# Small tiles padded to whole lines of 128 bytes, so that every tile in SBUF begins at a multiple of 128 bytes

## The chip, the core and the metric

The kernel runs on one core of one Trainium2 chip. The metric is the device time of one execution in microseconds (us); the median of three runs before the change is 1016.87 us. Engines carry the names of the profile: PE is TensorE's matmul stream, PEld its weight loads, DVE is VectorE, ACT is ScalarE, POOL is GpSimd, SP is the queue that issues the DMAs. For each matmul PE reads two operands from SBUF: the stationary one (128 columns, read by the weight load) and the moving one (256 or 512 columns, streamed through the array).

## What is computed

A transformer trunk of two layers on 256 rows of 1024 float32 channels. Each layer is a SwiGLU, a token mixer with 16 heads of three kinds, and a second SwiGLU, each with a norm before and after it:

```python
def swiglu(h, w_gate, w_up, w_down):
    return (jax.nn.silu(h @ w_gate) * (h @ w_up)) @ w_down

def reference(x, norm_gains, w_ffn_gate, w_ffn_up, w_ffn_down, w_in, w_out, diff_lambda, diff_subln_gain):
    for layer in range(DEPTH):
        g = norm_gains[layer]
        h = rmsnorm(x, g[0])
        x = x + 0.5 * rmsnorm(swiglu(h, w_ffn_gate[layer, 0], w_ffn_up[layer, 0], w_ffn_down[layer, 0]), g[1])
        h = rmsnorm(x, g[2])
        x = x + rmsnorm(token_mixer(h, w_in[layer], w_out[layer], diff_lambda[layer], diff_subln_gain[layer], layer), g[3])
        h = rmsnorm(x, g[4])
        x = x + 0.5 * rmsnorm(swiglu(h, w_ffn_gate[layer, 1], w_ffn_up[layer, 1], w_ffn_down[layer, 1]), g[5])
    return x
```

D_MODEL is 1024, D_FF is 2816. The four SwiGLUs hold 138 MB of the weights, the two mixers the rest of some 180 MB, all of it read from HBM once.

## The kernel before

**Weights.** `half` loads a piece of 128 x 1024 float32 into one of five buffers `raw`; ACT copies it into a float32r tile (`L271`, the high part) and DVE writes the difference into a second one (`L274`, the low part). The two tiles are one of ten `ring` buffers, here called ring0 to ring9; each takes its turn when it has been free for longest.

**Products.** A product of two float32 matrices is three matmuls (`mm3`): high by high, high by low, low by high, each with its own weight load. All matmuls come from one line of a helper, `mm`, `L356`, so the profile tells them apart by operands: `ps<-xt,ring` (rows `xt` moving, 256 columns, weights `ring` stationary: gate and up of a SwiGLU, queries and keys), `ps<-ring,xt` (weights moving, 256 columns, rows stationary: the first blocks of a SwiGLU, values), `ps<-ring,h` (weights moving, 512 columns, hidden values `h` stationary: down and the mixer's output). In a name of the profile the moving operand stands first.

**Order.** Each operation has a written-down duration; `Program.run` orders them for each engine by a list schedule before anything runs. The order is fixed in the program; only the semaphores' times differ from run to run.

**Where tiles lie.** Every tile is taken from one pool, `P1`, and gets an address at its first use, behind the tile before it. The program as built puts each at a multiple of 32 bytes and no more, so that a small tile such as `sm` (four float32 values, 16 bytes; 24 of them) shifts all the tiles behind it:

```python
    SM = Slots(P1, "sm", 24, [128, 4])
```

Addresses below are bytes from the start of a partition's row, as the program was built. A tile's row of 1024 float32 values is 4096 bytes, and all slices that PE reads begin at a multiple of 256 bytes from their tile's start, so the tile's start decides the slice's offset to a line.

Of the kernel before, what the change touches and what calls it, by code (L numbers as in the profile page):

```python
# [8 lines left out]
F32 = mybir.dt.float32  # L9
# [26 lines left out]
LAST_ORDER = ((9, 0), (6, 1), (10, 0), (7, 1), (8, 1), (9, 1), (10, 1))  # L36

C_IDENT, C_NEGU, C_NEG1, C_BLK, C_MASK = 0, 128, 256, 384, 512
C_BIAS = 768
# [29 lines left out]
class Slots:  # L69
    """Buffers of one kind (each one or more tiles); the one that has been free for longest goes first."""  # L70

# [12 lines left out]
class Buf:  # L84
    """A buffer from its first operation to its last one."""

# [12 lines left out]
class Program:  # L99
    """Operations with their dependencies, put in an order for each engine by a list schedule over  # L100
    estimated times (most urgent first), then traced in that order."""

# [119 lines left out]
def trunk(tc, x, norm_gains, w_gate, w_up, w_down, w_in, w_out, dlam, subln, consts, out):  # L222
# [16 lines left out]
    QS = Slots(P1, "q", N_QS, [128, 256])  # L239
    SM = Slots(P1, "sm", 24, [128, 4])  # L240
    GPO = Slots(P1, "gpo", 1, [128, D])
# [8 lines left out]

# [1 line left out]
    class Half:  # L252
# [4 lines left out]
    def half(pieces, cut=2):  # L257
        """Loads [128, 1024] and splits it exactly into two float32r parts."""
        h = Half()
        raw, h.ring = Buf(RAW), Buf(RNG, F32R)  # L260

        def load():
            for view, ap in pieces:
                nc.sync.dma_start(view(raw.t), ap)

        ld = op("DMA", 1.5, load, [prev[0]], [raw], lag=DMA_LAG)
        hi, lo = [], []
        w = 1024 // cut
        for s in (slice(w * c, w * (c + 1)) for c in range(cut)):
            def fhi(s=s):  # L270
                nc.scalar.activation(h.ring.t[0][:, s], raw.t[:, s], AF.Copy)  # L271

            def flo(s=s):
                nc.vector.tensor_tensor(h.ring.t[1][:, s], raw.t[:, s], h.ring.t[0][:, s].bitcast(F32), OP.subtract)  # L274

            hi.append(op("ACT", act_us(w, False), fhi, [ld] + hi[-1:] + last_hi, [raw, h.ring]))
            lo.append(op("DVE", dve_us(w), flo, [hi[-1]], [raw, h.ring]))
        last_hi[:] = hi[-1:]
        h.ready = lo
        prev[0] = ld  # L280
        return h
# [31 lines left out]

# [1 line left out]
    xs = P1.tile([128, 2, D], F32, name="xs")  # L315
    xr = x[0].rearrange("(t p) d -> p t d", p=128)
    cst = P1.tile([128, N_CONST], F32, name="cst")
    lamt = P1.tile([128, DEPTH, 4, 32], F32, name="lamt")
    gcol = P1.tile([128, DEPTH], F32, name="gcol")
    small = P1.tile([128, 2], F32, name="small")  # L320
    mhalf, epsc = small[:, 0:1], small[:, 1:2]
    nlam = P1.tile([128, DEPTH], F32, name="nlam")
    maskb = P1.tile([128, 256], BF16, name="maskb")
# [11 lines left out]
    def warm():  # L335
        """Work on zeros that brings the tensor engine to its full clock while the first loads run."""
        z, p = Buf(H2, BF16), Buf(PS)
        o = op("POOL", 0.2, lambda: nc.gpsimd.memset(z.t, 0.0), [], [z])

        def pe():  # L340
            for _ in range(N_WARM):
                mm(p.t, z.t[:, 0:128], z.t, True, True)

        op("PE", WARM_US, pe, [o], [z, p])
# [33 lines left out]

# [1 line left out]
    def sumsq(src, after, bufs, scale, psum):  # L380
        """Means of squares of the two halves of rows, in two columns."""
        v = Buf(SM)
        os = []
        for i in range(2):
            j = Buf(JK, BF16)

            def f(i=i, j=j):
                nc.scalar.activation(j.t, src(i), AF.Square, scale=scale, accum_out=v.t[:, i:i + 1])  # L388

            os.append(op("ACT", act_us(512, psum, 1), f, after[i], bufs[i] + [v, j]))  # L390
        return v, os
# [10 lines left out]
    def residual(T, accs, done, g, half_, final=False):  # L402
        """Norm of a sub-layer's output (token block T), added to the residual rows."""
        v, sq = sumsq(lambda i: accs[i].t, done, [[a] for a in accs], 1.0 / 16 if half_ else 1.0 / 32, True)
        r, orr = rstd(v, sq, 4 * EPS if half_ else EPS)
        res = []
        for i in range(2):
            y = Buf(ES)

            gb, gv, gl = g[i]  # L410

            def fy(i=i, y=y, gv=gv):
                nc.vector.tensor_tensor(y.t, accs[i].t, gv(), OP.mult)  # L413

            def fx(i=i, y=y):
                s = HALF[i]
                nc.vector.scalar_tensor_tensor(xs[:, T, s], y.t, r.t[:, 0:1], xs[:, T, s], OP.mult, OP.add)

            oy = op("DVE", dve_us(512), fy, done[i] + [gl], [accs[i], gb, y])
            ox = op("DVE", 0.66, fx, [oy, orr], [y, r])  # L420
            res.append(ox)
            if final:
                op("DMA", 0.8, lambda i=i: nc.sync.dma_start(out[0, TS(T), HALF[i]], xs[:, T, HALF[i]]), [ox])
        return res

    def normed(T, xo, g):
        """Normed rows of block T, in two halves."""
        v, sq = sumsq(lambda i: xs[:, T, HALF[i]], [[o] for o in xo], [[], []], 1.0 / 32, False)
# [12 lines left out]
    class XT:  # L441
        """Transposed normed rows in two float32r parts; done[T][b]: the ends for block T, chunk half b."""

# [31 lines left out]
    def wk(h, k):  # L475
        """Columns of contraction chunk k from two half tiles of 4 chunks each."""
        v = [t.rearrange("p (k c) -> p k c", k=4)[:, k % 4, :] for t in h[k // 4].ring.t]
        return v[0], v[1]
# [4 lines left out]
    def rows_op(p, c0, xt, T, hs, first):  # L483
        """p[:, c0:c0+256] = rows of block T times the 256 columns of tile hs; two steps."""
        o = None
# [7 lines left out]

# [1 line left out]
    def ffn(l, s, xt, na, turn1, g, final, nxt, pre):  # L495
        """turn1(): traces the second block's transposes; returns what follows the sub-layer."""
        wg, wu, wd = w_gate[l, s], w_up[l, s], w_down[l, s]
# [126 lines left out]

# [1 line left out]
    def mixer(l, xt, turn1, g, nxt, o_cst, o_misc):  # L626
# [22 lines left out]
        def qk(i):  # L649
            """Projects queries and keys of pair i, scaled, and splits both in two float32r parts.  # L650
            Differential pairs (4 maps of 32 channels): each map gets a tile with its two parts twice, in such
            an order that one pass over 128 partitions carries the four products. The others: the stationary
            side of head b has its high part on its own partitions and the low part on the other head's, the
            moving side its high part on both, so that two passes carry three products."""
            kind, n = PAIRS[i]
# [53 lines left out]
        def products(p, i, b, blocks, between=lambda: None):  # L709
            """Scores of head b of pair i; blocks: (output columns, stationary columns, moving columns)."""  # L710
            r = qk_[i]
            for n, (co, cs, cm) in enumerate(blocks):
                mm(p.t[:, co], r["s"][b].t[:, cs], r["m"][b].t[:, cm], n == 0)
            between()
            for co, cs, cm in blocks:
                mm(p.t[:, co], r["s"][b].t[HB[b], cs], r["l"].t[HB[b], cm], False, True)
# [4 lines left out]
        def scores(i, r0, n, h, den, d0):  # L721
            """exp(scores + bias - max) in rows, [block 1: keys 256 | block 0: keys 128], and the sums."""
            qk = qk_[i]
# [48 lines left out]
        def pair(i):  # L772
            """Generator: one stage at each next()."""
            kind, n = PAIRS[i]
# [18 lines left out]
            elif kind == "diff":  # L793
                es = []
                for b in range(2):
# [3 lines left out]
                    def comb(e1=e1, e2=e2, den=den, r=r):  # L799
                        nc.vector.reciprocal(r.t, den.t)  # L800
                        nc.vector.tensor_scalar(r.t[:, 2:4], r.t[:, 2:4], nlam[:, l:l + 1], None, OP.mult)
# [152 lines left out]

# [1 line left out]
    prev[0] = gp[0][2]  # L956
# [10 lines left out]
    def misc():  # L967
# [15 lines left out]
        pr = P1.tile([128, DEPTH, 2, 32], F32, name="pr")  # L983
        sm = P1.tile([128, DEPTH, 2], F32, name="sm")
        ex = P1.tile([128, DEPTH, 2], F32, name="ex")

# [4 lines left out]
        def f2():  # L991
            nc.vector.tensor_tensor(nlam, ex[:, :, 0], ex[:, :, 1], OP.subtract)
            for l in range(DEPTH):
# [63 lines left out]
```

## Time and profile before

| | |
|---|---|
| three runs | 1016.26, 1016.87, 1017.44 us |
| span of the profiled execution, first to last instruction | 1013.1 us |
| what lies around that span, by the median | 3.8 us |
| PE, PEld busy | 996.0, 923.9 us |
| DVE, ACT, POOL busy | 632.0, 581.9, 33.4 us |
| share of the chain that ended last: PE, ACT, DVE, DMA | 87%, 7%, 2%, 1% |
| DMA, mean | 181 GB/s, queue 59% busy |

Busy time of PE is the union of its matmuls' spans, from the start of one to its last result; neighbours overlap. How fast PE runs is seen in the distance from one matmul's start to the next, its pace, and that is read from rows of the timeline: the length of a row of n equal matmuls, less the duration of one, divided by n - 1. The core's mean granted TensorE clock was 0.998 of 2.4 GHz.

### The profile page before, as it was taken

The numbers are of one execution on the slowest core, as the hardware profiler recorded it, in microseconds if no ns is written. First come the engines' busy times: TensorE is split into PE (matmuls) and PEld (weight loads), VectorE is DVE, ScalarE is ACT, GpSimd is POOL, SyncE is SP. The second block draws the span as 40 slices with busy tenths as digits, with TensorE's granted clock in tenths as the row PEclk, the third lists the DMA queues.
The fourth block names the chain that finished last, engine by engine and source line by source line (L and its number), as shares of the span: only waits on it lengthen the run. The fifth ranks groups of instructions, "written<-read, shape, count | busy, mean of one in ns | idle before, by whom it ended". The sixth has DMA issues, their size and how long they took to land.

```text
span 1013.1 us, 18111 instructions
## 1 busy us (share of the span) xinstructions
PE 996.0 (98%) x7146; PEld 923.9 (91%) x7146; DVE 632.0 (62%) x1123; ACT 581.9 (57%) x1133; POOL 33.4 (3%) x58
## 2 busy tenths in 40 slices
PE   7999999999999999999999999999999999999997
PEld 6999999898888999999899999999998789999996
DVE  6755544778898745454685554448799776545433
ACT  6654443769996544443665444447899765444431
POOL 0000000100002000000000000002000020000000
PEclk9999999999999999999999999999999999999999
DMA  8986664684335766654577656557732547665531
GB/s 275 321 286 191 185 181 140 200 246 110 113 116 177 239 190 185 192 182 149 168 232 226 194 181 202 149 160 233 211 104 86 160 152 233 186 195 179 165 104 42
DMA packets 157574, 183.38 MB, mean 181 GB/s; under 512 B 6064, under 2 KB 141488, under 8 KB 157360
## 3 DMA queue, kind: packets, MB, share of 16 engines
q1 hardware_dynamic: 157488, 182.21, 59.0%
q8 instruction: 56, 0.92, 0.4%
q14 instruction: 30, 0.25, 0.1%
HBM read 181.14 MB, written 1.05 MB: 180 GB/s over the span
## 4 chain that ended last, share of the span: by engine, by line
PE 87%; ACT 7%; DVE 2%; issue 1%; DMA 1%; POOL 0%; SPq 0%; DVEq 0%; POOLq 0%; ACTq 0%
PE ps L356 86%; ACT q L679 2%; ACT ring L271 1%; ACT q L695 1%; PE ps L462 1%; DMA raw<-in_w_ffn_gate 1%; ACT e L746 1%; DVE q L683 0%; ACT sn L824 0%; ACT sn L825 0%; ACT sn L823 0%; DVE ring L274 0%; POOL sm L398 0%; ACT junk L388 0%; DVE q L699 0%
## 5 line engine op out<-in xcount | busy, mean ns | idle before, releaser
L271 ACT ACTIVATE ring<-raw 128x512 fp32r<-128x512 f32 (+1 forms) x552 | 367.0, 705 | 324.5 <-issue 221.6
L274 DVE TENSOR_TENSOR ring<-raw,ring 128x512 fp32r<-128x512 f32 (+1 forms) x552 | 414.2, 787 | 202.0 <-ACT ring L271 197.0
L356 PE MATMUL ps<-xt,ring 128*128 128x256 f32 x4320 | 519.7, 281 | 0.0
L356 PEld LDWEIGHTS ps<-xt,ring 128*128 128x128 f32 x4320 | 513.5, 189 | 4.8 <-issue 1.7
L356 PE MATMUL ps<-ring,h 128*128 128x512 f32 x1248 | 297.6, 393 | 0.0
L356 PEld LDWEIGHTS ps<-ring,h 128*128 128x128 f32 x1248 | 230.0, 188 | 47.4 <-issue 0.3
L356 PE MATMUL ps<-ring,xt 128*128 128x256 f32 x1056 | 131.1, 283 | 2.7 <-DVE xt L468 1.8
L356 PEld LDWEIGHTS ps<-ring,xt 128*128 128x128 f32 x1056 | 127.8, 190 | 4.0 <-DVE xt L468 2.5
L564 DVE TENSOR_TENSOR e<-ps,e 128x512 f32<-128x512 f32 x37 | 25.6, 691 | 111.0 <-PE ps L356 111.0
L397 POOL TENSOR_SCALAR sm<-sm 128x1 f32<-128x1 f32 x24 | 15.7, 653 | 928.7 <-ACT junk L388 715.8
L565 ACT ACTIVATE h<-e 128x512 fp32r<-128x512 f32 x37 | 23.2, 627 | 25.4 <-DVE e L564 25.4
L413 DVE TENSOR_TENSOR e<-ps,gpo 128x512 f32<-128x512 f32 x24 | 16.4, 687 | 21.2 <-ACT junk L388 20.9
L388 ACT ACTIVATE junk<-ps 128x512 bf16<-128x512 f32 x24 | 14.3, 595 | 26.4 <-PE ps L356 25.5
L356 PE MATMUL ps<-q,q 128*128 128x256 f32 (+3 forms) x128 | 25.9, 295 | 3.2 <-DVE q L684 2.1
L695 ACT ACTIVATE q<-ps 64x256 fp32r<-64x256 f32 x72 | 27.1, 376 | 0.8
L562 ACT ACTIVATE e<-ps 128x512 f32<-128x512 f32 x37 | 21.9, 592 | 9.8 <-PE ps L356 9.8
L356 PEld LDWEIGHTS ps<-q,q 128*128 128x128 f32 (+1 forms) x128 | 19.4, 187 | 8.6 <-issue 1.7
L436 DVE SCALAR_TENSOR_TENSOR pt<-xs,sm,gpr 128x512 f32<-128x512 f32 x24 | 17.0, 748 | 14.5 <-DMA gpr<-in_norm_gains 8.4
L566 DVE TENSOR_TENSOR h<-e,h 128x512 fp32r<-128x512 f32 x37 | 25.3, 684 | 0.0
L746 ACT ACTIVATE e<-sn,sm 128x256 f32<-128x256 f32 (+1 forms) x56 | 24.7, 446 | 0.1
L679 ACT ACTIVATE q<-ps 32x256 fp32r<-32x256 f32 x64 | 23.9, 374 | 0.9
L699 DVE SCALAR_TENSOR_TENSOR q<-ps,q 64x256 fp32r<-64x256 f32 x48 | 20.2, 421 | 1.1
(82 smaller groups left out, 387.7 us busy)
## 6 DMA issues: line engine op xcount, KB each, us to landing
raw<-in_w_ffn_gate SPq DMA_DIRECT2D x88, 512.0 KB, 4.5
raw<-in_w_ffn_up SPq DMA_DIRECT2D x88, 512.0 KB, 4.8
raw<-in_w_ffn_down SPq DMA_DIRECT2D x88, 512.0 KB, 4.2
raw<-in_w_in SPq DMA_DIRECT2D x40, 512.0 KB, 4.9
raw<-in_w_out SPq DMA_DIRECT2D x16, 512.0 KB, 3.6
raw<-in_w_in SPq DMA_DIRECT2D x16, 256.0 KB, 4.0
gpr<-in_norm_gains SPq DMA_DIRECT2D x6, 512.0 KB, 5.4
gpo<-in_norm_gains SPq DMA_DIRECT2D x6, 512.0 KB, 5.6
```

The lines of the kernel that those rows point to most:

```text
L271: nc.scalar.activation(h.ring.t[0][:, s], raw.t[:, s], AF.Copy)
L274: nc.vector.tensor_tensor(h.ring.t[1][:, s], raw.t[:, s], h.ring.t[0][:, s].bitcast(F32), OP.subtract)
L356: nc.tensor.matmul(o, a, b, start=start, stop=stop, skip_group_check=True)
L436: nc.vector.scalar_tensor_tensor(h.t, xs[:, T, HALF[i]], r.t[:, 0:1], gv(), OP.mult, OP.mult)
L562: a = op("ACT", act_us(512, True), lambda p=p: nc.scalar.activation(sg.t, p.t, AF.Silu), os[-1:], [p, sg])
L564: m_ = op("DVE", dve_us(512), lambda p=p: nc.vector.tensor_tensor(sg.t, p.t, sg.t, OP.mult), os[-1:] + [a], [p, sg])
L565: o1 = op("ACT", act_us(512, False), lambda: nc.scalar.activation(bh.t, sg.t, AF.Copy), [m_], [sg, bh])
L566: o2 = op("DVE", dve_us(512), lambda: nc.vector.tensor_tensor(bl.t, sg.t, bh.t.bitcast(F32), OP.subtract), [o1], [sg, bh, bl])
L679: nc.scalar.activation(b.t[QB[e], :], p.t[QB[m], :256], AF.Copy, scale=scale)
L695: nc.scalar.activation(bs[b].t[HB[b ^ e], :], p.t[HB[b], :256], AF.Copy, scale=scale)
L699: nc.vector.scalar_tensor_tensor(lo[b].t[HB[b ^ other], :], p.t[HB[b], :256], scale, bs[b].t[HB[b], :].bitcast(F32), OP.mult, OP.subtract)
L746: nc.scalar.activation(e.t[:, SEG[a]], sn.t[:, SEG[a]], AF.Exp, bias=mn.t[:, a:a + 1], scale=-1.0, accum_out=den.t[:, d0 + a:d0 + a + 1])
```

## The change

Each tile that is smaller than a line becomes 32 float32 values wide (`LINE`, 128 bytes) and is used in its first columns as before. Since all the other tiles are a multiple of 128 bytes, every tile then begins at a multiple of 128 bytes. The docstrings and comments that are removed too change no instruction.

```diff
+LINE = 32
...
-    SM = Slots(P1, "sm", 24, [128, 4])
+    SM = Slots(P1, "sm", 24, [128, LINE])
...
-    gcol = P1.tile([128, DEPTH], F32, name="gcol")
-    small = P1.tile([128, 2], F32, name="small")
+    gcol = P1.tile([128, LINE], F32, name="gcol")
+    small = P1.tile([128, LINE], F32, name="small")
     mhalf, epsc = small[:, 0:1], small[:, 1:2]
-    nlam = P1.tile([128, DEPTH], F32, name="nlam")
+    nlam = P1.tile([128, LINE], F32, name="nlam")
...
-                        nc.vector.reciprocal(r.t, den.t)
+                        nc.vector.reciprocal(r.t[:, 0:4], den.t[:, 0:4])
...
-        sm = P1.tile([128, DEPTH, 2], F32, name="sm")
-        ex = P1.tile([128, DEPTH, 2], F32, name="ex")
+        sm = P1.tile([128, LINE], F32, name="sm")[:, 0:2 * DEPTH].rearrange("p (l f) -> p l f", l=DEPTH)
+        ex = P1.tile([128, LINE], F32, name="ex")[:, 0:2 * DEPTH].rearrange("p (l f) -> p l f", l=DEPTH)
...
-            nc.vector.tensor_tensor(nlam, ex[:, :, 0], ex[:, :, 1], OP.subtract)
+            nc.vector.tensor_tensor(nlam[:, 0:DEPTH], ex[:, :, 0], ex[:, :, 1], OP.subtract)
```

In the two programs as built, every engine and the DMA queue has the same instructions in the same order on the same buffers, with the same waits; only line numbers (by three) and addresses differ. The pool ends at byte 219,920 of a row before and 222,720 now. Where the larger tiles begin, as the remainder by 128:

| tiles | before | after |
|---|---|---|
| `xs`, `cst`, `lamt` | 0 | 0 |
| `maskb`, `identb`, `trir` | 96 | 0 |
| `xt`, both parts | 96 | 0 |
| ring0, ring1, both parts | 96 | 0 |
| ring2 to ring9, both parts | 32 | 0 |
| `h` (12), `e` (5), `gpr`, `gpo` | 32 | 0 |
| `pt`: two, two | 96, 32 | 0 |
| `raw`: 0, 1 to 3, 4 | 64, 96, 32 | 0 |
| `q`: 14, 2 | 32, 0 | 0 |
| `sn`: three | 32, 64, 96 | 0 |

PE's matmuls are all in the trace, in the program's order, so each run of them in the timeline can be given its buffers. In the second SwiGLU of the first layer (numbers in brackets: remainder by 128):

| run of matmuls begins at, us | moving | stationary |
|---|---|---|
| 352.64, the first 48 | `xt` (96) | ring0, ring1 (96) |
| 369.52 | `xt` (96) | ring6, 7, 4, 5 (32) |
| 380.83 | ring0, ring1 (96) | `h` (32) |
| 386.43 | `xt` (96) | ring8, 9, 2, 3 (32) |
| 397.32 | ring6, ring7 (32) | `h` (32) |
| 461.90 | ring0, ring1 (96) | `h` (32) |
| 464.70 | `xt` (96) | ring8, 9, 6, 7 (32) |

## Rows read from the trace of the kernel before

**Rows 1.** The page: busy shares; granted clock by slice; shares of the last chain.

```profile
PE 996.0 (98%) x7146; PEld 923.9 (91%) x7146; DVE 632.0 (62%) x1123; ACT 581.9 (57%) x1133; POOL 33.4 (3%) x58
PEclk9999999999999999999999999999999999999999
PE 87%; ACT 7%; DVE 2%; issue 1%; DMA 1%; POOL 0%; SPq 0%; DVEq 0%; POOLq 0%; ACTq 0%
```

**Rows 2.** Chain that ended last: by line; long pieces: start, us, what, matmuls.

```profile
by line: PE ps L356 85.7%; ACT q L679 2.3%; issue 1.3%; ACT ring L271 1.2%; ACT q L695 0.9%; PE ps L462 0.8%; DMA raw<-in_w_ffn_gate 0.7%; ACT e L746 0.7%; DVE q L683 0.4%; ACT sn L824 0.4%; ACT sn L825 0.4%; ACT sn L823 0.4%; DVE ring L274
...
2.58 7.14 DMA raw<-in_w_ffn_gate
...
28.97 167.44 PE ps L356 x1188
196.41 0.87 PE ps L462 x8
...
348.63 157.64 PE ps L356 x1110
...
535.74 158.33 PE ps L356 x1110
...
846.43 160.25 PE ps L356 x1122
```

**Rows 3.** Groups by shape in 28.97:196.41 (first two) and 846.43:1006.68 (last two).

```profile
L356 PE MATMUL ps<-xt,ring 128*128 128x256 f32 x936 | 111.4, 280 | 0.0
L356 PE MATMUL ps<-ring,h 128*128 128x512 f32 x252 | 59.4, 391 | 0.0
...
L356 PE MATMUL ps<-xt,ring 128*128 128x256 f32 x864 | 102.6, 280 | 0.0
L356 PE MATMUL ps<-ring,h 128*128 128x512 f32 x258 | 60.8, 392 | 0.0
```

**Rows 4.** Groups of the page: matmuls and weight loads, mean ns of one.

```profile
L356 PE MATMUL ps<-xt,ring 128*128 128x256 f32 x4320 | 519.7, 281 | 0.0
L356 PEld LDWEIGHTS ps<-xt,ring 128*128 128x128 f32 x4320 | 513.5, 189 | 4.8 <-issue 1.7
L356 PE MATMUL ps<-ring,h 128*128 128x512 f32 x1248 | 297.6, 393 | 0.0
```

**Rows 5.** Timeline of PE, 352.7:358.3, then 369 to 465: start, us, run of matmuls.

```profile
352.64 5.91 PE L356 MATMUL ps<-xt,ring 128*128 128x256 f32 x48
...
369.52 11.47 PE L356 MATMUL ps<-xt,ring 128*128 128x256 f32 x96
380.83 5.76 PE L356 MATMUL ps<-ring,h 128*128 128x512 f32 x24
386.43 11.05 PE L356 MATMUL ps<-xt,ring 128*128 128x256 f32 x96
397.32 5.62 PE L356 MATMUL ps<-ring,h 128*128 128x512 f32 x24
...
461.90 2.96 PE L356 MATMUL ps<-ring,h 128*128 128x512 f32 x12
464.70 11.05 PE L356 MATMUL ps<-xt,ring 128*128 128x256 f32 x96
```

**Rows 6.** Groups by shape, ACT and DVE, whole span: mean ns of one.

```profile
L271 ACT ACTIVATE ring<-raw 128x512 fp32r<-128x512 f32 x448 | 257.4, 623 | 205.9 <-issue 139.2 <-PE ps L356 44.5 <-DMA raw<-in_w_ffn_gate 10.0
L388 ACT ACTIVATE junk<-xs 128x512 bf16<-128x512 f32 x24 | 14.9, 623 | 7.2 <-DVE xs L417 5.8 <-DMA xs<-in_x 1.3
L436 DVE SCALAR_TENSOR_TENSOR pt<-xs,sm,gpr 128x512 f32<-128x512 f32 x24 | 17.0, 748 | 14.5 <-DMA gpr<-in_norm_gains 8.4 <-POOL sm L398 6.2
L417 DVE SCALAR_TENSOR_TENSOR xs<-e,sm,xs 128x512 f32<-128x512 f32 x24 | 16.9, 747 | 3.3 <-POOL sm L398 3.3
```

**Rows 7.** Busy us by stretch; DMA share and GB/s at the end.

```profile
210.00:345.00 135.00, 132.31 (x986) 120.48 (x985) 111.07 (x269) 111.89 (x268) 6.10 (x8) 1.00 0.51 151
360.00:500.00 140.00, 140.00 (x1006) 131.65 (x1005) 71.09 (x98) 62.11 (x100) 0.86 (x2) 1.00 0.59 178
```

**Rows 8.** DMA issues: KB each, median us to landing.

```profile
raw<-in_w_ffn_gate SPq DMA_DIRECT2D x88, 512.0 KB, 4.5
cst<-in_consts SPq DMA_DIRECT2D x1, 1600.0 KB, 12.0
```

## Prediction

> **What bounds the kernel.** I read the page first. PE is busy for 98% of the span at the full clock of 2.4 GHz (no slice of PEclk is below 9), DVE and ACT for 62% and 57% [rows 1]. The chain that ended last is PE for 87%, and 85.7% of the span is the one matmul line [rows 2]. Its four long pieces are the four SwiGLUs: 167.44 + 157.64 + 158.33 + 160.25 = 643.7 us in which PE never waits for anybody. So in two thirds of the span the only question is how fast PE takes one matmul after another. DVE and ACT work for half of such a stretch (71 and 62 of 140 us) and the DMA engines for 0.59 of it; in the mixer's stretch both are busy for some 111 of 135 us, and the long chain pieces on PE are shorter there [rows 7]. Mean durations (281 and 393 ns) are latencies and overlap [rows 4]; pace is what counts, the step from start to start.
>
> Pace comes from the timeline [rows 5]: a row's length less one latency, by the number of steps. The run of 96 matmuls at 386.43 gives (11.05 - 0.28)/95 = 113.4 ns, the one at 369.52 gives (11.47 - 0.28)/95 = 117.8 ns, and the 48 at 352.64 give (5.91 - 0.28)/47 = 119.8 ns. All are `ps<-xt,ring` with 256 columns at the same clock. 256 columns at 2.4 GHz are 106.7 ns, so 6.7 to 13.1 ns of each are something else. With 512 columns (213.3 ns of array time) the run at 380.83 gives (5.76 - 0.39)/23 = 233.3 ns and the one at 397.32 (5.62 - 0.39)/23 = 227.4 ns: 14 to 20 ns over.
>
> What differs between these runs is the buffers, and by the table of buffers their offset: 119.8 and 233.3 are the runs on ring0 and ring1 (96 bytes past a line), the others those on buffers 32 past one. The excesses step by nearly the same amount, 6 to 7 ns, which is 16 columns at 2.4 GHz or 64 bytes of float32. I take this as PE reading SBUF in pieces of fixed places, so that a stream which begins inside a piece costs up to one or two more reads. The row does not say which piece, and no large PE stream in this trace begins at 0.
>
> **The change part by part.** *Instructions*: same list, same order, same waits; the padded tiles are read and written in the same columns. Cost: 0. *ACT and DVE*: a group that reads a tile at offset 0 takes what others take: ACT on `xs` (0) 623 ns, on `raw` (32 to 96) 623 ns; DVE writing `xs` (0) 747 ns, writing `pt` (96 and 32) 748 ns [rows 6]. Cost: 0, and neither is the bound in a SwiGLU [rows 7]. *DMA*: landing rows now begin on a line. The one load that already lands at 0, `cst`, moved 1600/12.0 = 133 KB per us, a weight load 512/4.5 = 114 [rows 8]; DMA stands on the chain only for the first 7.14 us [rows 2], so at most 7.14 x (1 - 114/133) = 1.0 us; the sizes differ, so I take 0.
>
> *PE*: the two operands of all the large streams move to 0. What a stream there costs is bounded from below by array time, 106.7 and 213.3 ns; from above, if 0 were no better than the worst offset seen, by 119.8 and 233.3. Inside these I look for the nearest row. The transposes' moving operand is the identity in `cst`, which is at 0 already: eight take 0.87 us, 109 ns each [rows 2]. They move 128 columns (53 ns), so it is their weight load of 128 columns that sets this pace, from `pt` at 96 or 32; so a weight load needs no more than 109 ns once the moving side is out of its way. With 256 columns the matmul needs 106.7. So I take **109 ns** for 256 columns. For 512 no row at 0 exists; the excess of 14 to 20 ns should lose about what the other loses, and I take the smallest excess that the 256-wide runs show, 6.7 ns: **220 ns**.
>
> The Trainium skill, "TensorE: Matmul & The Clock Gate", section Back-to-back issue gap, gives N/2.4 + 2.5 ns for a warm gap: 109.2 and 215.7 here. No run of this trace is that quick; by it the four pieces would be some 4 us shorter than by my values.
>
> **The sum.** The four pieces hold 1188 + 1110 + 1110 + 1122 = 4530 matmuls [rows 2]. The first has 936 of 256 columns and 252 of 512, the last 864 and 258, the two between 864 and 246 (1110 less the same 864) [rows 3]; together 3528 and 1002. At 109 and 220 ns: 384.6 + 220.4 = 605.0 us instead of 643.7, so 38.7 us or 6.0% less. The matmul line holds 0.857 x 1013.1 = 868 us of the chain, so 224.5 us outside these pieces; 6.0% of that is 13.5. There ACT and DVE are near (112 and 111 of 135 us [rows 7]) and take over part of the chain when PE is quicker, so I count two thirds: 9.0. Sum: -47.7 us on the profiled span, 1013.1 to 965.4; with the 3.8 us that lie between this span and the median of the runs, **969 us**.
>
> **Rivals.**
> 1. *Only the worse offset goes.* 0 behaves as 32 does at its best: 113.4 and 227.4 ns everywhere. For it: these are the quickest paces that exist in the trace, and 117.8 and 113.4 both occur on buffers at 32 (the quicker one at 386.43 and 464.70, both right after a run on ring0 and ring1 [rows 5]), so something besides the offset, how the two streams fall in step, has a part. Against: it would give offset 0 no merit over 32. 3528 x 0.1134 + 1002 x 0.2274 = 627.9, so -15.8; the rest 2.5% of 224.5, two thirds of it, -3.7: 997 us.
> 2. *Array time alone remains.* 106.7 and 213.3 ns: 590.1, so -53.6; the rest 8.3%, two thirds, -12.5: 951 us. For it: the excess goes in steps, which can all vanish. Against: the transposes' 109.
> 3. *No change.* The pace hangs on the buffer's place or partner, not on its offset: ring0 and ring1 are also those that lie next to `xt`. 1017 us. The buffers' places hardly change, so this would leave both paces. The Trainium skill, "SBUF — State Buffer", section Specifications (TRN2), speaks for this one: it gives cachelines of 16 bytes, and all tiles begin at a multiple of 32 before as well, so by that rule a start at 0 changes nothing. That the trace has several paces for one shape is what that rule doesn't explain.
> 4. *Slower.* The 119.8 ns run has both operands at 96, the 113.4 and 117.8 runs have them at 96 and 32. If it is equal offsets that make the weight reads and the moving reads meet, all streams now have equal offsets, and all go at the worst pace: 3528 x 0.1198 + 1002 x 0.2333 = 656.4, so +12.7; the rest 2.0% of 224.5, all on PE, +4.4: 1034 us. Against: with 512 columns the equal pair (32 and 32) is the quicker one, 227.4 against 233.3 for 96 and 32 [rows 5]. It decides from a 256-wide pace of 117.4 ns on, where, with 512 columns staying near the middle of their two paces (229), the four pieces take their 643.7 us again.
>
> **How the numbers follow.** The forecast (256-wide pace near 109, 512-wide between 214 and 224) has a chance of 0.48, rival 1 0.24, rival 2 0.10, rival 3 0.08, rival 4 0.10. The first three are faster: 0.82. Runs of this kernel differ by 0.1%, so 0.2% (2 us) is about what can be told from no change: same 0.08, slower 0.10. The range takes the forecast and rivals 1 and 2 with a few us at either end, **946 to 1001 us**; what is left out is rivals 3 and 4.
>
> **What would show it.** Right: runs of 96 matmuls in the timeline near 10.6 us instead of 11.05 to 11.47, runs of 24 near 5.4 to 5.5, and the same length whichever ring buffers they use; the four chain pieces near 150 us each; ACT, DVE and POOL groups at the same means; a mixer that shrinks by less than its share. Rival 1 shows runs of 96 at 11.05 everywhere. Rival 3 keeps the difference between ring0, ring1 and the others. Rival 4 shows 11.7 everywhere. I would be wrong most likely by the 256-wide pace: 1 ns of it is 3.5 us in the four pieces.

## The result and the profile after

The changed kernel takes **1025.74 us** (median of 4 runs, 1025.29 to 1025.92); the kernel before took 1016.59 beside it (4 runs). The ratio is 1.0094, with a 95% interval of 1.0082 to 1.0106: slower by 0.9%. The prediction was 969 us, range 946 to 1001; both the sign and the size are wrong.

The page of the kernel after: busy time by engine, and groups with busy us and mean ns. All its line numbers are three higher.

```profile
PE 1007.9 (98%) x7146; PEld 938.0 (92%) x7146; DVE 632.4 (62%) x1123; ACT 582.2 (57%) x1133; POOL 33.7 (3%) x58
...
L359 PE MATMUL ps<-xt,ring 128*128 128x256 f32 x4320 | 531.3, 283 | 0.0
L359 PEld LDWEIGHTS ps<-xt,ring 128*128 128x128 f32 x4320 | 524.8, 192 | 4.7 <-issue 1.7
L359 PE MATMUL ps<-ring,h 128*128 128x512 f32 x1248 | 296.1, 392 | 0.0
```

Against [rows 1, 4]: ACT, DVE and POOL are where they were; PE grew by 11.9 us. The 4,320 matmuls with `xt` moving went from 519.7 to 531.3 us, and the 1,248 of 512 columns from 297.6 to 296.1. One group lost, the other gained a little. The third large group, the 1,056 matmuls of 256 columns with `xt` stationary, went from 131.1 to 133.1. The span went from 1013.1 to 1023.5 us. The span of before belongs to a quick execution: in every run with both on record the time lies 1.7 to 1.8 us above the span, so that execution should have taken about 1014.9 us (an estimate), 2 less than the median. The change cost 9.2 us by the medians, not 10.4.

The chain that ended last, after: start, us, what. These are the four pieces of [rows 2], and the transposes behind one of them.

```profile
29.47 169.64 PE ps L359 x1188
...
352.36 159.66 PE ps L359 x1110
...
541.79 159.69 PE ps L359 x1110
701.48 0.87 PE ps L465 x8
...
854.72 162.38 PE ps L359 x1122
```

They sum to 651.4 us against 643.7. The transposes still take 0.87 us, though their stationary operand now begins on a line.

The timeline of PE, after, in the SwiGLU of [rows 5]: start, us, run of matmuls.

```profile
356.31 11.68 PE L359 MATMUL ps<-xt,ring 128*128 128x256 f32 x96
367.82 5.63 PE L359 MATMUL ps<-ring,h 128*128 128x512 f32 x24
373.29 11.68 PE L359 MATMUL ps<-xt,ring 128*128 128x256 f32 x96
384.80 5.63 PE L359 MATMUL ps<-ring,h 128*128 128x512 f32 x24
```

From the start of a run to that of the next, divided by its matmuls, is the pace: (367.82 - 356.31)/96 = 119.9 ns and (373.29 - 367.82)/24 = 227.9 ns, whatever the ring buffers. Before, a run of 96 took 11.05 or 11.47 us, or 11.57 where half of it was on ring0 and ring1, and one of 24 took 5.62 to 5.65 or 5.76. So the 256-column runs now go at the worst pace that the kernel before knew, and the 512-column runs close to its best.

### The profile page after: what moved, and what is told of

Its sections match the earlier page's. It is cut to its first block, busy times and chain, and to the rows that moved or that the text cites. A ratio compares the mean times of both kernels' runs of the same rounds, so it can differ in the third digit from the quotient of the medians.

```text
span 1023.5 us, 18111 instructions
## 1 busy us (share of the span) xinstructions
PE 1007.9 (98%) x7146; PEld 938.0 (92%) x7146; DVE 632.4 (62%) x1123; ACT 582.2 (57%) x1133; POOL 33.7 (3%) x58
## 4 chain that ended last, share of the span: by engine, by line
PE 88%; ACT 6%; DVE 2%; issue 1%; DMA 1%; POOL 0%; SPq 0%; DVEq 0%; POOLq 0%; ACTq 0%
PE ps L359 86%; ACT q L682 2%; ACT ring L274 1%; PE ps L465 1%; DMA raw<-in_w_ffn_gate 1%; ACT e L749 1%; ACT q L698 1%; DVE q L686 0%; DVE ring L277 0%; ACT junk L391 0%; ACT sn L827 0%; POOL sm L401 0%; DVE q L702 0%; ACT sn L828 0%; PE ps L536 0%
## 5 line engine op out<-in xcount | busy, mean ns | idle before, releaser
L359 PE MATMUL ps<-xt,ring 128*128 128x256 f32 x4320 | 531.3, 283 | 0.0
L359 PEld LDWEIGHTS ps<-xt,ring 128*128 128x128 f32 x4320 | 524.8, 192 | 4.7 <-issue 1.7
L359 PE MATMUL ps<-ring,h 128*128 128x512 f32 x1248 | 296.1, 392 | 0.0
L359 PE MATMUL ps<-ring,xt 128*128 128x256 f32 x1056 | 133.1, 286 | 1.8 <-DVE xt L471 1.5
```

The source lines that it names most:

```text
L359: nc.tensor.matmul(o, a, b, start=start, stop=stop, skip_group_check=True)
```

## Three theories, and what tells them apart

What the two traces have in common is not an offset but a difference. With offsets by 256 bytes instead of 128, before: `xt` 96, ring0 and ring1 96, ring2 to ring9 160, `h` 160 (one of the twelve 32); after: all 0. At 256 columns (96, 96) before and (0, 0) after both go at 120 ns, and (96, 160) at 113 or 118. At 512 columns (160, 160) and (0, 0) go at 227, (96, 160) at 233.

- **T1**: the pace goes by the moving operand's offset less the stationary one's, modulo 256. Equal is bad for 256 columns and good for 512. Absolute alignment is nothing.
- **T2**: each operand's own place in a line of 128 bytes counts (the reading of the prediction); 0 happens to be as bad as 96.
- **T3**: the buffers' places or partners count.

## The experiments

**1. Matmuls alone (m1_sweep, one execution).** The whole computation is left out. Each pair (m, s) of byte offsets behind a multiple of 256 has 48 matmuls of 256 columns and 24 of 512:

```python
for i in range(count):
    a = m // 4 + (256 * (i % 4) if n == 256 else 512 * (i % 3))
    b = s // 4 + 128 * (i % 8)
    mm(ps[n // 256 - 1][:, 0:n], sta[:, b:b + 128], mov[:, a:a + n], i == 0, i == count - 1)
```

> The whole computation is left out (x is copied to the output); after 32 warming matmuls of 512 columns, for each pair of byte offsets (moving operand, stationary operand) 48 matmuls of 256 columns and 24 of 512 run back to back, every pair on source lines of its own. T1 (the pace goes by the moving offset less the stationary offset, in bytes, modulo 256): (0,0), (0,256), (32,32), (96,96) and (160,160) all give about 120.0 ns at 256 columns and 226.7 at 512; (96,160) gives 113 to 118 and 233.3; other differences lie between these, and a pair with a shifted start, as (0,64) and (32,96), gives the same as another of the same difference. T2 (the pace goes by each operand's place within a line of 128 bytes): (0,0) and (96,96) are alike by chance, (32,32) and (160,160) are quicker than 120 at 256 columns, and (0,128) gives the same as (0,0). T3 (the operands' distance or bank in SBUF, not the offset): all pairs alike.

The timeline of PE, matmuls alone. The pairs are (0,0) on L35 and L36; (0,16) on L37; (0,64) on L41 and L42; (0,128) on L45 and L46; (0,160) on L47 and L48; (0,256) on L53 and L54; (32,96) on L57 and L58; (96,160) on L63 and L64; (160,32) on L69; (64,0) on L71 and L72.

```profile
20.87 5.92 PE L35 MATMUL ps<-mov,sta 128*128 128x256 f32 x48
26.62 5.63 PE L36 MATMUL ps<-mov,sta 128*128 128x512 f32 x24
32.09 5.84 PE L37 MATMUL ps<-mov,sta 128*128 128x256 f32 x48
...
54.50 5.60 PE L41 MATMUL ps<-mov,sta 128*128 128x256 f32 x48
59.94 5.75 PE L42 MATMUL ps<-mov,sta 128*128 128x512 f32 x24
...
76.78 5.86 PE L45 MATMUL ps<-mov,sta 128*128 128x256 f32 x48
82.48 5.74 PE L46 MATMUL ps<-mov,sta 128*128 128x512 f32 x24
88.06 5.92 PE L47 MATMUL ps<-mov,sta 128*128 128x256 f32 x48
93.82 5.76 PE L48 MATMUL ps<-mov,sta 128*128 128x512 f32 x24
...
121.83 5.92 PE L53 MATMUL ps<-mov,sta 128*128 128x256 f32 x48
127.58 5.64 PE L54 MATMUL ps<-mov,sta 128*128 128x512 f32 x24
...
144.27 5.82 PE L57 MATMUL ps<-mov,sta 128*128 128x256 f32 x48
149.92 5.75 PE L58 MATMUL ps<-mov,sta 128*128 128x512 f32 x24
...
178.03 5.82 PE L63 MATMUL ps<-mov,sta 128*128 128x256 f32 x48
183.68 5.75 PE L64 MATMUL ps<-mov,sta 128*128 128x512 f32 x24
...
211.65 5.93 PE L69 MATMUL ps<-mov,sta 128*128 128x256 f32 x48
...
223.01 5.82 PE L71 MATMUL ps<-mov,sta 128*128 128x256 f32 x48
228.66 5.67 PE L72 MATMUL ps<-mov,sta 128*128 128x512 f32 x24
```

A row less one matmul's 0.28 us, over 47: 120.0 ns at (0,0) and at (0,256), so the pattern repeats after 256 bytes; 118.7 at (0,128), where 512 columns take 5.74 us instead of 5.63, so it does not repeat after 128. (32,96) and (96,160), which differ alike, have equal rows at both widths; (64,0), the opposite difference, has 5.82 and 5.67 us. (32,32), (96,96) and (160,160) gave 5.91, 5.91 and 5.90 us, like (0,0). T2 and T3 fail. T1 holds at 512 columns in every pair; at 256 columns two pairs have another pace than others of their difference. (0,64), of the same difference as (96,160), ran at 5.60 us, 113.2 ns, and (160,32), of the same difference as (0,128), at 5.93 us, 120.2 ns. So the difference alone does not always fix the pace. The kernel before had both paces of the first case too, 11.05 and 11.47 us on buffers with the same offsets [rows 5]. Unequal is not always better either: (0,160), a difference of 96, takes 120.0 ns at 256 columns and 233.5 at 512, the slow pace at both.

**2. One operand moved, or all (four kernels).** In e1_xt64 the two tiles of `xt` begin 64 bytes later; in e3_h64 the tiles of `h`; in e2_all32 everything moves by 32 bytes; e9_before_xt160 makes the edit of e1_xt64 in the kernel before, so that `xt` equals ring2 to ring9 instead of ring0 and ring1.

```diff
...
-    XTS = Slots(P1, "xt", 1, [128, KC, SEQ], 2)
+    XTS = Slots(P1, "xt", 1, [128, KC * SEQ + 64], 2, 16)   # e1_xt64, e9_before_xt160: used from column 16 on
...
-    H2 = Slots(P1, "h2", 12, [128, 512])
+    H2 = Slots(P1, "h2", 12, [128, 576], 1, 16)             # e3_h64
...
+    P1.tile([128, 8], F32, name="pad")                      # e2_all32, ahead of all others
```

> The kernel after, with the tiles of xt alone begun 64 bytes behind a multiple of 256; ring and h stay at multiples. T1: the 5,376 matmuls of 256 columns with xt and ring fall from 119.9 to 113 to 118 ns, the 1,248 of 512 columns stay at 226.7 to 228: 1025.7 - 5376 x (2 to 6.7 ns) = 990 to 1015 us, faster than the kernel after and than the kernel before. T2 (offset 0 in a line of 128 bytes is bad by itself): ring stays at 0, so at most half of that goes, 1010 to 1026. T3 (place): no change, 1025.

> The kernel after, with 32 bytes put ahead of all tiles, so that every tile begins 32 bytes behind a multiple of 128 and all moving and stationary offsets stay equal. T1 (only the difference counts): 1025.7, no change against the kernel after, 120.0 and 226.7 ns. T2 (an offset of 32 was among the quick ones of the kernel before, and 0 and 96 are bad): faster than the kernel after by 5 to 35 us, 990 to 1020. That alignment to 32 or 128 bytes matters in itself and is good: slower than the kernel after.

> The kernel after, with the h2 tiles alone (the stationary side of the 1,248 matmuls of 512 columns) begun 64 bytes behind a multiple of 256. T1: these go from about 228 to 233.3 ns, +5 to 7 us; the matmuls of 256 columns stay at 119.9 or take another locked pace after the changed runs; 1025.7 + 5 to 7 = 1031 to 1033 us if they stay. T2: the pair is no longer both at offset 0, so no slower, 1020 to 1026. T3: no change, 1025.

> The kernel before, not aligned at all, with xt alone moved by 64 bytes, from 96 to 160 modulo 256, so that it equals the 16 tiles of ring2 to ring9 and differs from those of ring0 and ring1 instead. T1: 3,552 of the 4,320 matmuls with xt moving go to 120.0 ns (from 116.6 in the mean), 768 from 120 to 117.8, the ones with xt stationary likewise (768 and 288): +12.3 - 1.7 + 1.9 - 0.6 = +12 us, 1027 to 1029 us, that is, the loss of the change without any tile being aligned. T2 (a place within a line of 128 bytes): xt goes from 96 to 32, ring unchanged, so faster or the same, 1000 to 1017 us.

| kernel | us, median | ratio to before (95%) |
|---|---|---|
| e1_xt64 | 1014.82 | 0.9982 (0.9973 to 0.9991) |
| e2_all32 | 1026.10 | 1.0093 (1.0080 to 1.0107) |
| e3_h64 | 1032.21 | 1.0152 (1.0138 to 1.0166) |
| e9_before_xt160 | 1023.41 | 1.0069 (1.0055 to 1.0082) |

The timelines of PE in the same SwiGLU. First e1_xt64:

```profile
386.70 11.47 PE L362 MATMUL ps<-xt,ring 128*128 128x256 f32 x96
398.01 5.64 PE L362 MATMUL ps<-ring,h 128*128 128x512 f32 x24
```

e2_all32:

```profile
390.93 11.68 PE L360 MATMUL ps<-xt,ring 128*128 128x256 f32 x96
402.44 5.63 PE L360 MATMUL ps<-ring,h 128*128 128x512 f32 x24
```

e3_h64:

```profile
393.55 11.66 PE L362 MATMUL ps<-xt,ring 128*128 128x256 f32 x96
405.04 5.77 PE L362 MATMUL ps<-ring,h 128*128 128x512 f32 x24
```

e9_before_xt160 (the second run of 96 has half its matmuls on ring0 and ring1):

```profile
390.08 11.67 PE L359 MATMUL ps<-xt,ring 128*128 128x256 f32 x96
401.59 5.63 PE L359 MATMUL ps<-ring,h 128*128 128x512 f32 x24
407.06 11.36 PE L359 MATMUL ps<-xt,ring 128*128 128x256 f32 x96
```

The first takes the 256-column pace to (398.01 - 386.70)/96 = 117.8 ns and leaves 512 columns alone: 2.1 ns by 5,376 matmuls (4,320 with `xt` moving, 1,056 with it stationary) are 11 us, and 10.9 were measured. The second changes nothing, as T1 says: no tile is aligned to more than 32 bytes and the time stays, where T2 has 990 to 1020. (T3 fails on the first and the third, for which it has no change.) The third puts 512 columns at 5.77 us and costs 6.5 us. The fourth brings most of the loss about in a kernel that keeps its unaligned tiles: 11.67 where there was 11.05 or 11.47. It lost 7 us and not 12. In part this is because matmuls on ring0 and ring1 gained more than I had reckoned: the run at 407.06 has 48 at 120 ns, so the other 48 take (11.36 - 0.28 - 48 x 0.120)/47 = 113.2 ns, the quicker pace again, not 117.8. At most some 2 of the 5 us are of this kind: the four SwiGLU pieces of its last chain took 650.5 us, 6.8 more than before, and their share of my reckoning is 8.7. The rest of the gap is not explained.

**3. Two paces for one difference (m2_states, m3_kicks, one execution each).** Both leave the computation out. A run of one unequal pair is set behind 12 matmuls of 512 columns at equal offsets and a short prelude.

```python
go(mm, 0, 0, 512, 12)     # equal offsets
go(mm, 0, 0, 192, 1)      # the prelude, here one matmul of 192 columns
go(mm, 0, 64, 256, 48)    # the run that is read
```

> The whole computation is left out. For each of six pairs of unequal offsets a run of 48 matmuls of 256 columns is set behind a prelude, which itself follows 12 matmuls of 512 columns at equal offsets: nothing; 24, 6 or 2 matmuls of 512 columns at a difference of 192; 12 at a difference of 64; one matmul of 64, 128, 192, 320 or 384 columns at equal offsets; 12 of 256 columns at equal offsets; four f32 matmuls of 128 columns. T1a (the two paces 113.3 and 117.8 ns of one pair are two locked states, chosen by what ran just before): the pair (0,64) runs at 117.8 without a prelude and at 113.3 behind the 512-column runs at a difference of 192; the two states hold for all 48. T1b (the pace at unequal offsets drifts, or depends on the buffers): no prelude changes it by more than 1 ns. If T1a holds, the open question is whether a single short matmul is enough to choose the quick state, and for which differences there is one.

> The whole computation is left out. Behind 12 matmuls of 512 columns at equal offsets stand preludes of one to 24 matmuls, then 32 matmuls of 256 columns at (64,0) or (0,64), or 16 of 512 columns at five pairs. One matmul of 192 columns at equal offsets set the quick state (113.3 ns) before. If the state is a place in time between the weight reads and the moving reads that one odd length shifts and that then holds itself (theory S): a 192-column matmul of the pair itself, and 64 + 192 columns of the pair in place of one of 256, set it too; in the middle of a slow run as well; lengths near 192 (176, 208) do so partly; a second one of 192 may undo it; four f32 matmuls or a run at equal offsets undo it. If instead the quick state needs the change of offsets at that matmul (theory E): only the preludes at equal offsets set it, 117.8 for all of the pair's own. At 512 columns S leaves open a state below 226.7, about 220; none would say that 226.7 is the least at this length.

Timeline of PE in m2_states, pair (0,64): without a prelude (L41), then behind one matmul of 192 columns (L143, L144).

```profile
24.08 5.82 PE L41 MATMUL ps<-mov,sta 128*128 128x256 f32 x48
...
389.81 0.25 PE L143 MATMUL ps<-mov,sta 128*128 128x192 f32 x1
389.90 5.63 PE L144 MATMUL ps<-mov,sta 128*128 128x256 f32 x48
```

One matmul of an odd length puts all 48 behind it on the quicker pace, (5.63 - 0.28)/47 = 113.8 with the first few in it, 113.3 in the later ones. The pairs (0,16), (0,32) and (96,0) had only one lasting pace each (that of the later half of a run), 118.3, 118.3 and 120.0 ns, whatever came before. (0,128) had two again: its 48 took 5.93 us without a prelude and 5.86 behind 24 matmuls of 512 columns at a difference of 192. I had expected a 512-column run at a difference of 192 to bring the quicker pace; at any of its three lengths it did not (117.8), while 12 of them at a difference of 64 did. Timeline of PE in m3_kicks, pair (0,64): behind two matmuls of 128 columns of the pair itself (L142), and behind 16 of its own at the slower pace and one of 192 (L163).

```profile
233.17 3.87 PE L142 MATMUL ps<-mov,sta 128*128 128x256 f32 x32
...
281.24 3.96 PE L163 MATMUL ps<-mov,sta 128*128 128x256 f32 x32
```

At (0,64) preludes of the pair's own set the quicker pace in all eight forms that stood at the start of a run (192; 64 + 192; 192 + 64; 128 + 128; 384; 160; 176; 208), but not in the middle of a slower run, and the four f32 matmuls took it away again. At (64,0) only 160 of these eight did. There one matmul of 192 columns at equal offsets had set it in m2_states; two of them did not, three did. At 512 columns no prelude brought a lasting pace under 226 ns; but (0,16) held two there as well, 16 matmuls in 3.79 us without a prelude and in 3.90 behind one of 384 columns at equal offsets, which is 226.7 and 234.0 ns. So theory S is right in that a pair can hold either pace, and E, that the offsets must change at that matmul, is wrong; but which length sets it I can only list.

**4. The quicker pace in the kernel (five kernels).** e5_xt192 has `xt` at 192 (difference 192, as in (0,64)) and all else at 0. e4_xt192_h64 has `h` at 64 as well. e6_split64 and e7_split128 write the first matmul of each gate step of e5_xt192 as two; e8_split_equal is e7_split128 with `xt` back at 0.

```diff
...
+if part == 0 and m == 0 and k == 0:
+    mm(p.t[:, 0:128], wh[:, c], xt.hi(k, slice(0, 128)), True)      # 64 in place of 128: e6_split64
+    mm(p.t[:, 128:256], wh[:, c], xt.hi(k, slice(128, 256)))
+    mm(p.t[:, 0:256], wh[:, c], xt.lo(k, slice(0, 256)))
+    mm(p.t[:, 0:256], wl[:, c], xt.hi(k, slice(0, 256)))
+    continue
...
```

> The kernel after, with xt begun 192 bytes and h2 64 bytes behind a multiple of 256, ring at 0: moving less stationary is 192 for the 4,320 matmuls with xt moving, 64 for the 1,056 with xt stationary, 192 for the 1,248 of 512 columns. T1a: the 512-column runs go at 233.3 ns and leave the next 256-column run in the quick state, 113.3: 1032.2 (h2 alone moved) - 4320 x 6.5 ns - 1056 x 2 ns = 1002 us. T1b: 117.8 ns instead, 1032.2 - 10.9 = 1021 us. T2 and T3: as the run with h2 alone moved, 1026 to 1032.

> The kernel after, with xt alone begun 192 bytes behind a multiple of 256 (moving less stationary 192 with xt moving, 64 with xt stationary, 0 at 512 columns). T1 with two states: behind 512-column runs at equal offsets the 256-column runs stay in the slow state, 117.8 ns, as with xt at 64: 1014 to 1016 us. If most runs fall into the quick state without help: 995 to 1005 us.

> As the run before (xt at 192), and in each gate step of both row blocks together the first matmul of 256 columns is written as one of 64 and one of 192 columns (37 more matmuls in all, the same result). State theory: this one odd length puts the run behind it into the quick state, 113.3 ns for about 3,900 of the 4,320: 1015 - 3900 x 4.5 ns + 37 x at most 0.06 us = 997 to 1001 us. If the state does not hold in the kernel (other runs and transposes between): 1013 to 1018 us.

> As the run before, split 128 and 128 columns. State theory, by the runs of matmuls alone, where both splits chose the quick state at this difference: 997 to 1001 us. If the choice hangs on the exact length: between that and 1017 us.

> The kernel after with its equal offsets kept (xt at 0), and the first matmul of each gate step of both row blocks together split in 128 and 128 columns as in the run with xt at 192. T1: at equal offsets there is one pace only, 120.0 ns, and the split costs its own 37 x about 0.11 us: 1028 to 1031 us. If the split itself were what gained, with any offsets: 1008 to 1016 us.

| kernel | us, median | ratio to before (95%) |
|---|---|---|
| e4_xt192_h64 | 1014.11 | 0.9984 (0.9975 to 0.9993) |
| e5_xt192 | 1014.33 | 0.9986 (0.9977 to 0.9995) |
| e6_split64 | 1018.59 | 1.0026 (1.0016 to 1.0036) |
| e7_split128 | **1004.52** | 0.9889 (0.9875 to 0.9902) |
| e8_split_equal | 1029.64 | 1.0135 (1.0121 to 1.0148) |

Timelines of PE again; a row's form is that of its first matmul. e5_xt192:

```profile
386.63 11.47 PE L362 MATMUL ps<-xt,ring 128*128 128x256 f32 x96
397.94 5.60 PE L362 MATMUL ps<-ring,h 128*128 128x512 f32 x24
```

e4_xt192_h64:

```profile
385.73 11.47 PE L362 MATMUL ps<-xt,ring 128*128 128x256 f32 x96
397.04 5.76 PE L362 MATMUL ps<-ring,h 128*128 128x512 f32 x24
402.64 11.06 PE L362 MATMUL ps<-xt,ring 128*128 128x256 f32 x96
```

e6_split64:

```profile
388.50 11.57 PE L362 MATMUL ps<-xt,ring 128*128 128x64 f32 x97
399.91 5.62 PE L362 MATMUL ps<-ring,h 128*128 128x512 f32 x24
```

e7_split128:

```profile
384.27 11.16 PE L362 MATMUL ps<-xt,ring 128*128 128x128 f32 x97
395.27 5.62 PE L362 MATMUL ps<-ring,h 128*128 128x512 f32 x24
```

e8_split_equal:

```profile
393.01 11.78 PE L362 MATMUL ps<-xt,ring 128*128 128x128 f32 x97
404.62 5.63 PE L362 MATMUL ps<-ring,h 128*128 128x512 f32 x24
```

From start to start a gate and up run of 96 takes 11.51 us in the kernel after, 11.31 in e5_xt192 (the slower pace, 117.8 ns), 11.61 in e8_split_equal (the split costs 0.10 us, by 37 of them 3.7; measured +3.9), 11.41 in e6_split64, and 395.27 - 384.27 = 11.00 in e7_split128. So with unequal offsets the split in 128 and 128 brings the quicker pace; the one in 64 and 192 does not in the kernel, though alone it did, and 1018.59 us is far from the 997 to 1001 expected; and with equal offsets the split is only a cost. In e4_xt192_h64 the runs went at both paces in turn, so that it came to neither of the two times expected, and what they gained the 512-column runs at 5.76 us took back. e7_split128 beats both kernels: by 1.1% the one before and by 21 us the one after.

## Why the prediction was wrong

**The step that failed** is "What differs between these runs is the buffers, and by the table of buffers their offset". It gave the offset of each operand the credit, and what the pace follows, up to the choice between two paces at some differences, is the difference of the two: e2_all32 moves every offset and changes nothing, e1_xt64 moves one operand and gives back 11 us. The step also passed over its own rows: 113.4 and 117.8 ns came from buffers with the same offsets, as rival 1 notes, so the offsets could not be all of it. The remainder by 128, by which I listed the tiles, is too coarse as well: at 512 columns (0,128) takes 5.74 us and (0,0) 5.63.

**The values 109 and 220 ns** came from that step and from the transposes. Offset 0 measured 119.9 and 227.9; the pace at 512 columns, which the sum let fall from 227.4 to 220, did not fall. The transposes kept their 109 ns when their stationary operand went from 96 or 32 to 0, so they said nothing of the effect of an offset at 256 columns. The Trainium skill, "TensorE: Matmul & The Clock Gate", section Back-to-back issue gap, gives N/2.4 + 2.5 ns, here 109.2 and 215.7, for what it calls the isolated gap, and says that a stream with a weight load for each matmul goes by both. No run here, all with such loads, shows these two values: the lowest lasting paces were 113.3 and about 226.5 ns.

**Rival 4 was the case**, with a chance of 0.10. Its mechanism's condition, equal offsets, is what the runs show, and its pace of 119.8 at 256 columns was right to 0.1 ns. Mis-sized was its 512-column term, 233.3 where 227.9 came; with that, 3528 x 0.1199 + 1002 x 0.2279 = 651.4 us, which is the sum of the four pieces. Why weight reads and moving reads should meet was not tested and stays a picture. What I held against it, that the equal pair is the quicker one at 512 columns, is true, and no objection: the two widths go opposite ways. The 119.9 ns lie above its threshold of 117.4, and the kernel is slower, as it says.

**The rest of the span**, -9.0 in the sum, came to +2.7 us by the profiled spans (10.4 less 7.7) and to +1.5 by the medians (9.2 less 7.7), with the same sign as the pieces. The 3.8 us that the sum adds around the span are 1.8 in the runs; the other 2 are the quick execution that the profile of before caught. **Instructions, ACT and DVE** at 0 were right: 582.2 and 632.4 us busy against 581.9 and 632.0 [rows 1]. DMA's 0 agrees with the pages: the gate weights' loads landed in 4.5 us before and after, and e2_all32, with no landing row on a line, took 1026.10 us against 1025.74.

**Rival 3** fell with experiment 2. The Trainium skill, "SBUF — State Buffer", section Specifications (TRN2), with its cachelines of 16 bytes taken as a rule for where a read begins, would make all these kernels equal, since every offset here is a multiple of 16; the measurement decides, and (0,16) with 118.3 ns against 120.0 at (0,0) shows a step that this rule does not have.

**Still open**: why a difference of 64, 128 or 192 bytes holds two paces, what fixes which one a run falls into (64 + 192 columns did it alone and not in the kernel), and what keeps 256 columns from going below 113.3 ns.

## What to carry to other kernels

When one shape of matmul shows several paces in a trace, tabulate the offsets of both operands together, modulo 256 bytes, before giving either the credit; here two rows of the kernel before, those at 352.64 and 386.43 [rows 5], were enough to suggest the pair. Aligning everything makes all pairs equal, which in this kernel helped streams of 512 columns by up to 6 ns each and cost those of 256 columns 2 to 7. A pad of 64 or 192 bytes on one operand of the 256-column streams, with the 512-column pairs left equal, is worth a run; 96 is not, by (0,160).

## What was not expected of the hardware

PE keeps a pace: one and the same pair ran 48 or 96 matmuls at 113.3 or at 117.8 ns, and one short matmul ahead of the run decided it. That was worth 10 us in the kernel (1014.33 to 1004.52), the 37 splits' own cost of about 3.7 us included.
